# The opening of a two-block network on one core: first two products in a written order

## The chip, the core and the metric

The kernel runs on one core of a Trainium2 chip. A core has five engines with a queue each: TensorE (PE in the profile; its weight loads are PEld), VectorE (DVE), ScalarE (ACT), GpSimd (POOL) and SyncE (SP), which here only issues DMA transfers. An engine works off its queue in order; engines wait for each other through semaphores. The metric is device time in microseconds (us); times before are the median of three runs.

## The reference

The reference is a network of two blocks on 256 tokens of 1024 features, in float32, with its parameters as inputs. What matters here is its very first step, a norm and one wide product:

```python
def rmsnorm(x, g):
    xf = x.astype(jnp.float32)
    y = xf * lax.rsqrt(jnp.mean(xf * xf, axis=-1, keepdims=True) + RMS_EPS)
    return (y * g.astype(jnp.float32)).astype(x.dtype)
...
        h = rmsnorm(x, norm_mix_g[l])
        p = h @ w_in[l]
```

The columns of `p` go to a sliding-window attention, to a chunkwise mLSTM and to its gates; `w_out`, a cross attention with a second input `mem`, a gated feed-forward net, a second block (conformer convolution, sparse attention, two more feed-forward nets) and norms between them follow. All of that is unchanged.

## The kernel before

x lies transposed in SBUF, eight tiles of 128 features by 256 tokens (`self.x`, profile name `xres`). Weights come in chunks of 256 columns (`w_in` chunk 0, 1, 2, ...), each as two transfers of 512 KB into one of four raw buffers (`wraw`). To keep float32 accuracy at a faster matmul rate, every operand is split into a high part (a cast by ACT, L243 for weights and L325 for x) and a low part (the rest, by DVE, L246 and L326). A product is three matmuls: high by high, high by low, low by high (`mm3`, L263 to L265). One chunk is 8 tiles by 2 column halves by 3, that is 48 matmuls.

The norm's inverse root isn't applied to x. Products run on x times gain, and the root of the mean square, one number for each token, is multiplied in when a product leaves PSUM. It is made thus: the squares are summed over features, PE sums them over partitions (`zb`), DVE forms the mean (`rv`, L368), POOL takes the inverse root by 13 small instructions (`rsqrt`, `rs_n` and `rt_n`), PE spreads it over partitions (`bcb`, L375) and ACT copies that to SBUF (`bc_x`). DVE needs `bc_x` to evacuate the first products.

In the opening, `openB` and `norm` go through the eight tiles: split a tile, square it (ACT, or POOL for tiles 1, 3 and 5), let POOL add the squares up (`sqa`), and multiply the tile's rows of chunk 0. All transfers are issued by SP: the first gain columns of `par`, then weights and x in turn. The first mixer's steps (`MIX_AT`: chunks, gates, attention heads) are written in the order of a table of times. That is the order of the program; a scheduler may still move instructions of each engine's queue against it, outside of stretches marked `manual_schedule`, where the engines named keep the written order.

`w_in` chunk 2 holds the keys and values of the attention: DVE takes them out as `akT` and `avT`, and PE transposes `avT` (`bt`, L560). The gates' small product (`wgp`, from the transfer `gw`), the first attention scores (`bs`) and chunk 9 follow on PE.

Of the kernel before, what the change touches and what calls it, by code (L numbers as in the profile page):

```python
# [17 lines left out]
P = 128  # L18
# [113 lines left out]
class Net:  # L132
    def __init__(self, ctx, tc, T, dbg=None):
# [11 lines left out]

        nc.sync.dma_start(self.par[:, 0:KT], T["par"][:, 0:KT])
        self.early = [(self.x[:, m : m + 2, :], T["x"][:, m : m + 2, :]) for m in range(0, KT, 2)]
        self.early += [None, None, (self.ident, T["ident"]), (self.par[:, KT:], T["par"][:, KT:])]
# [18 lines left out]
    def plan(self, items):  # L167
        self.items = items
        self.stream = [(i, j) for i, item in enumerate(items) for j in range(len(self.sizes(item[0])))]
        self.data = [([], []) for _ in items]  # L170
        self.loaded = self.ready = self.used = 0
        self.run_ahead()
# [46 lines left out]
    def load(self, i, j):  # L219
        name, idx, _ = self.items[i]  # L220
        n = self.sizes(name)[j]
        raw = self.wp.tile([P, 1024], F32, name="wraw", tag="wraw", bufs=NRAW)[:, 0:n]
        self.nc.sync.dma_start(raw, self.T[name][idx][:, j * 1024 : j * 1024 + n])
        self.data[i][0].append(raw)
        for e in self.early[0:2]:
            if e:
                self.nc.sync.dma_start(*e)
        self.early = self.early[2:]
# [4 lines left out]
    def high(self, i, j):  # L233
        name, idx, k = self.items[i]
# [7 lines left out]
        hi, lo = both[:, 0, :], both[:, 1, :]  # L242
        self.nc.scalar.copy(hi, raws[j])  # L243

        def low():
            self.nc.vector.tensor_tensor(lo, raws[j], hi.bitcast(F32), op=ALU.subtract)  # L246
            pv = both.rearrange("p i (k c) -> p i k c", k=kh)
            prs.extend(pv[:, :, c, :] for c in range(kh))

        return low  # L250
# [23 lines left out]
    def linB(self, out, w, c0, c1, xx, nk=KT):  # L274
        for k in range(nk):
            self.mm3(out, w[k][:, :, c0:c1], xx[:, k], k == 0, k == nk - 1)

# [215 lines left out]
    def mixer(self, pool, mem):  # L493
# [29 lines left out]
        have, accs = set(), []  # L523
# [8 lines left out]
        def inp(c):  # L532
            nonlocal rb, rc
            if c == 0:
                b, step = self.openB(lambda: self.chunk("w_in", 0, room=0), xx)
                rc, _ = self.norm(lambda m: self.x[:, m, :], "g_mix", xx, step, (1, 3, 5))
                have.add("rc")
            elif c in (7, 8):
# [1214 lines left out]
```

## Time and profile before

| what | us |
|---|---|
| median of three runs (lowest, highest) | 1106.34 (1105.1, 1106.71) |
| the profiled execution | 1106.33 |
| its span, first to last instruction | 1104.5 |
| PE busy | 1063.6 (96%) |
| DVE busy | 803.6 (73%) |
| ACT busy | 598.2 (54%) |
| POOL busy | 138.9 (13%) |

The span is what the profile covers; the time of a run is a little longer. Busy is the time in which an engine had an instruction under way. PE's share leaves 40.9 us in which it stood. The profile's rows give start and duration, the engine, the line of the kernel, output and inputs by tile names, and, in brackets, how long the engine had been idle and what ended that.

### The profile page before, as it was taken

Reading aid. Unit: us, or ns where it says so; the run is one execution under the profiler, and the core shown is the slowest. Engines: PE = TensorE matmul, PEld = TensorE weight load, DVE = VectorE, ACT = ScalarE, POOL = GpSimd, SP = SyncE. Lnnn points to the kernel's source line nnn. Section 1 sums busy time; section 2 is a strip of 40 time slices with the busy share of each in tenths; the row PEclk is TensorE's granted clock in tenths of the full one; section 3 lists DMA queues with packets and bytes.
Section 4 is the critical chain, followed back from the end, with each engine's and each line's share of the span. In section 5 each row is a group of like instructions: output and inputs, shape, how many; then the busy total and the mean of one; then the engine's idle time right before and its main releaser. Section 6 shows DMA issues by size and latency. Waiting matters only on the chain.

```text
span 1104.5 us, 19673 instructions
## 1 busy us (share of the span) xinstructions
PE 1063.6 (96%) x7448; PEld 972.9 (88%) x7448; DVE 803.6 (73%) x1647; ACT 598.2 (54%) x1119; POOL 138.9 (13%) x343
## 2 busy tenths in 40 slices
PE   6899999999999999997789999999999999999998
PEld 6899999999999988885788888889999898888887
DVE  5886667768888865787877777765668748777763
ACT  5774556566666643311556666544365846666530
POOL 5120003012000000314030000012333103000000
PEclk9999999999999999998699999999999999999999
DMA  7744444435555654646165555755254034656670
GB/s 237 226 153 154 135 134 155 150 115 187 190 189 181 211 174 149 195 125 185 61 206 198 189 191 180 222 180 163 77 179 147 2 103 162 191 189 189 179 208 21
DMA packets 55414, 178.98 MB, mean 162 GB/s; under 512 B 9112, under 2 KB 11032, under 8 KB 55320
## 3 DMA queue, kind: packets, MB, share of 16 engines
q1 hardware_dynamic: 53400, 172.23, 49.3%
q0 software_dynamic: 1920, 5.50, 2.0%
q8 instruction: 58, 0.95, 0.3%
q14 instruction: 36, 0.29, 0.1%
HBM read 175.55 MB, written 2.16 MB: 161 GB/s over the span
## 4 chain that ended last, share of the span: by engine, by line
PE 84%; DVE 6%; DMA 3%; ACT 3%; POOL 2%; issue 2%; SPq 0%; ACTq 0%; DVEq 0%; POOLq 0%
PE pb L271 28%; PE pb L272 14%; PE pb L263 9%; PE pb L264 9%; PE pb L265 9%; PE pb L1034 3%; DVE cy L1096 2%; DMA wraw<-in_w_in_dram 1%; ACT wpr L243 1%; DVE wpr L246 1%; PE bt L1079 1%; PE bh L1357 1%; DVE xx L326 1%; DVE xres L443 1%; PE zb L1133 1%
## 5 line engine op out<-in xcount | busy, mean ns | idle before, releaser
L246 DVE TENSOR_TENSOR wpr<-wraw,wpr 128x1024 fp32r<-128x1024 f32 (+1 forms) x304 | 367.4, 1212 | 173.6 <-ACT wpr L243 171.0
L243 ACT CAST wpr<-wraw 128x1024 fp32r<-128x1024 f32 (+1 forms) x304 | 313.4, 1033 | 202.7 <-PE pb L272 95.1
L271 PE MATMUL pb<-xx,wpr 128*128 128x512 f32 x840 | 292.9, 392 | 0.0
L272 PE MATMUL pb<-xx,wpr 128*128 128x256 f32 x840 | 234.8, 280 | 0.0
L271 PEld LDWEIGHTS pb<-xx,wpr 128*128 128x128 f32 x840 | 157.7, 188 | 33.8
L271 PE MATMUL pb<-fhs,wpr 128*128 128x512 f32 x528 | 186.0, 394 | 0.0
L272 PEld LDWEIGHTS pb<-xx,wpr 128*128 128x128 f32 x840 | 157.8, 188 | 0.0
L272 PE MATMUL pb<-fhs,wpr 128*128 128x256 f32 x528 | 147.3, 279 | 0.0
L263 PE MATMUL pb<-xx,wpr 128*128 128x256 f32 x456 | 130.6, 290 | 8.7 <-ACT xx L325 8.6
L264 PE MATMUL pb<-xx,wpr 128*128 128x256 f32 x456 | 131.2, 288 | 2.5 <-DVE xx L326 2.4
L265 PE MATMUL pb<-xx,wpr 128*128 128x256 f32 x456 | 129.8, 285 | 0.0
L271 PEld LDWEIGHTS pb<-fhs,wpr 128*128 128x128 f32 x528 | 99.0, 187 | 23.2
L272 PEld LDWEIGHTS pb<-fhs,wpr 128*128 128x128 f32 x528 | 99.0, 188 | 0.0
L263 PEld LDWEIGHTS pb<-xx,wpr 128*128 128x128 f32 x456 | 87.5, 194 | 10.5 <-ACT xx L325 9.2
L264 PEld LDWEIGHTS pb<-xx,wpr 128*128 128x128 f32 x456 | 88.6, 194 | 4.0 <-DVE xx L326 3.3
L265 PEld LDWEIGHTS pb<-xx,wpr 128*128 128x128 f32 x456 | 88.5, 194 | 0.0
L263 PE MATMUL pb<-yy,wpr 128*128 128x256 f32 x256 | 74.0, 289 | 2.0 <-ACT yy L1175 2.0
L264 PE MATMUL pb<-yy,wpr 128*128 128x256 f32 x256 | 73.0, 285 | 0.0
L265 PE MATMUL pb<-yy,wpr 128*128 128x256 f32 x256 | 72.8, 285 | 0.0
L917 ACT COPY ft<-pb 128x256 f32<-128x256 f32 x105 | 38.7, 370 | 53.3 <-PE pb L272 53.3
L1096 DVE SCALAR_TENSOR_TENSOR cy<-cuz,par,cy 128x240 f32<-128x240 f32 (+14 forms) x120 | 55.2, 461 | 3.8
L263 PEld LDWEIGHTS pb<-yy,wpr 128*128 128x128 f32 x256 | 49.4, 193 | 2.4 <-ACT yy L1175 2.3
(422 smaller groups left out, 1952.4 us busy)
## 6 DMA issues: line engine op xcount, KB each, us to landing
wraw<-in_up_dram SPq DMA_DIRECT2D x44, 512.0 KB, 4.0
wraw<-in_up2a_dram SPq DMA_DIRECT2D x44, 512.0 KB, 4.4
wraw<-in_up2b_dram SPq DMA_DIRECT2D x44, 512.0 KB, 3.8
wraw<-in_w_in_dram SPq DMA_DIRECT2D x22, 512.0 KB, 4.5
wraw<-in_n_in_dram SPq DMA_DIRECT2D x20, 512.0 KB, 4.1
wraw<-in_wkv_dram SPq DMA_DIRECT2D x16, 512.0 KB, 4.2
wraw<-in_dn_dram SPq DMA_DIRECT2D x16, 512.0 KB, 3.7
wraw<-in_c_in_dram SPq DMA_DIRECT2D x16, 512.0 KB, 4.0
```

The source lines that it names most:

```text
L243: self.nc.scalar.copy(hi, raws[j])
L246: self.nc.vector.tensor_tensor(lo, raws[j], hi.bitcast(F32), op=ALU.subtract)
L263: mm(out, left[:, 0], right[:, 0], start=start, stop=False, skip_group_check=True)
L264: mm(out, left[:, 0], right[:, 1], start=False, stop=False, skip_group_check=True)
L265: mm(out, left[:, 1], right[:, 0], start=False, stop=stop, skip_group_check=True)
L271: mm(out, left[:, 0], right, start=start, stop=False, skip_group_check=True)
L272: mm(out[:, 0], left[:, 1], right[:, 0], start=False, stop=stop, skip_group_check=True)
L326: nc.vector.scalar_tensor_tensor(lo, src, g, hi.bitcast(F32), op0=ALU.mult, op1=ALU.subtract)
L443: self.nc.vector.tensor_tensor(self.x[:, m, :], acc[m // 2][:, (m % 2) * S : (m % 2) * S + S], self.x[:, m, :], op=ALU.add)
L917: nc.scalar.copy(t, b[:, 1])
L1034: nc.tensor.matmul(b, raw[k // 4][:, k % 4, c], xg[:, k, :], start=(k == 0), stop=(k == KT - 1))
L1096: nc.vector.scalar_tensor_tensor(y, us[m][:, 0 : S - t], tap(m, t), y, op0=ALU.mult, op1=ALU.add)
```

## The change

The first two products get a function of their own, `opening`, under `manual_schedule` for PE, DVE and ACT. x and the first columns of `par` are issued by ACT. PE multiplies 18 times a cleared tile. The first weight is split in halves, and within chunk 0 all high-by-high matmuls of four tiles come first, then high by low, then low by high. Chunk 1 follows, then the squares: all by ACT, each summed by PE at once (16 matmuls in place of 4), and the root is asked for behind that. The preloading of weights no longer begins in `plan`.

```diff
@@ -142,10 +142,6 @@
         self.x = self.cp.tile([P, KT, S], F32, name="xres")
         self.par = self.cp.tile([P, NPAR], F32, name="par")
         self.ident = self.cp.tile([P, P], F32, name="ident")
-        nc.sync.dma_start(self.par[:, 0:KT], T["par"][:, 0:KT])
-        self.early = [(self.x[:, m : m + 2, :], T["x"][:, m : m + 2, :]) for m in range(0, KT, 2)]
-        self.early += [None, None, (self.ident, T["ident"]), (self.par[:, KT:], T["par"][:, KT:])]
         self.ones = self.cp.tile([P, 1], F32, name="ones")
         nc.vector.memset(self.ones, 1.0)
         self.zero = self.cp.tile([P, 1], F32, name="zero")
@@ -169,7 +165,6 @@
         self.stream = [(i, j) for i, item in enumerate(items) for j in range(len(self.sizes(item[0])))]
         self.data = [([], []) for _ in items]
         self.loaded = self.ready = self.used = 0
-        self.run_ahead()
 
     @staticmethod
     def sizes(name):
@@ -222,15 +217,17 @@
         raw = self.wp.tile([P, 1024], F32, name="wraw", tag="wraw", bufs=NRAW)[:, 0:n]
         self.nc.sync.dma_start(raw, self.T[name][idx][:, j * 1024 : j * 1024 + n])
         self.data[i][0].append(raw)
-        for e in self.early[0:2]:
-            if e:
-                self.nc.sync.dma_start(*e)
-        self.early = self.early[2:]
 
     def convert(self, i, j):
         self.high(i, j)()
 
     def high(self, i, j):
+        both, raw = self.pair(i, j)
+        self.nc.scalar.copy(both[:, 0, :], raw)
+        return lambda: self.nc.vector.tensor_tensor(both[:, 1, :], raw, both[:, 0, :].bitcast(F32), op=ALU.subtract)
+    def pair(self, i, j):
         name, idx, k = self.items[i]
         n = self.sizes(name)[j]
         kh = n // P if name[:2] == "dn" else k // 2
@@ -239,15 +236,9 @@
             both = self.fp.tile([P, 2, 1024], F32R, name="wfi", tag="wfi", bufs=2)
         else:
             both = self.wp.tile([P, 2, 1024], F32R, name="wpr", tag="wpr", bufs=NHI)[:, :, 0:n]
-        hi, lo = both[:, 0, :], both[:, 1, :]
-        self.nc.scalar.copy(hi, raws[j])
-        def low():
-            self.nc.vector.tensor_tensor(lo, raws[j], hi.bitcast(F32), op=ALU.subtract)
-            pv = both.rearrange("p i (k c) -> p i k c", k=kh)
-            prs.extend(pv[:, :, c, :] for c in range(kh))
-        return low
+        pv = both.rearrange("p i (k c) -> p i k c", k=kh)
+        prs.extend(pv[:, :, c, :] for c in range(kh))
+        return both, raws[j]
 
     def chunk(self, name, idx, **ahead):
         assert self.items[self.used][:2] == (name, idx), (self.items[self.used], name, idx)
@@ -274,6 +265,76 @@
     def linB(self, out, w, c0, c1, xx, nk=KT):
         for k in range(nk):
             self.mm3(out, w[k][:, :, c0:c1], xx[:, k], k == 0, k == nk - 1)
+    def opening(self, gname):
+        nc, T = self.nc, self.T
+        mm = nc.tensor.matmul
+        nc.gpsimd.memset(self.yy[:, 0, 0].bitcast(F32), 0.0)
+        b, cold = [self.bank(), self.bank()], self.bank()
+        zb = self.zbank()
+        engines = {mybir.EngineType.PE, mybir.EngineType.DVE, mybir.EngineType.Activation}
+        with self.tc.manual_schedule(engines=engines):
+            nc.scalar.dma_start(self.par[:, 0:KT], T["par"][:, 0:KT])
+            for m in range(0, KT, 2):
+                nc.scalar.dma_start(self.x[:, m : m + 2, :], T["x"][:, m : m + 2, :])
+            while self.loaded < NRAW:
+                self.load(*self.stream[self.loaded])
+                self.loaded += 1
+            nc.sync.dma_start(self.ident, T["ident"])
+            nc.sync.dma_start(self.par[:, KT:], T["par"][:, KT:])
+            for _ in range(18):
+                mm(cold[:, 0:S], self.yy[:, 0, 0, 0:P], self.yy[:, 0, 0], start=True, stop=True)
+            w = self.data[0][1]
+            def weights(p, halves):
+                both, raw = self.pair(*self.stream[p])
+                n = raw.shape[1] // halves
+                cs = [slice(i * n, i * n + n) for i in range(halves)]
+                for c in cs:
+                    nc.scalar.copy(both[:, 0, c], raw[:, c])
+                    yield
+                for c in cs:
+                    nc.vector.tensor_tensor(both[:, 1, c], raw[:, c], both[:, 0, c].bitcast(F32), op=ALU.subtract)
+                    yield
+                self.ready += 1
+            def rows(m):
+                self.split_g(self.x[:, m, :], self.col(gname, m), self.xx[:, m])
+            def products(ks):
+                for lo, ro in ((0, 0), (0, 1), (1, 0)):
+                    for k in ks:
+                        for i in range(2):
+                            mm(b[i][:, 0:S], w[k][:, lo, i * P : i * P + P], self.xx[:, k, ro],
+                               start=(k == 0 and lo + ro == 0), stop=(k == KT - 1 and lo == 1), skip_group_check=True)
+            first = weights(0, 2)
+            next(first)
+            rows(0)
+            rows(1)
+            next(first)
+            rows(2)
+            rows(3)
+            for _ in first:
+                pass
+            for _ in weights(1, 1):
+                pass
+            products(range(4))
+            for m in range(4, KT):
+                rows(m)
+            products(range(4, KT))
+            for p in (2, 3):
+                for _ in weights(p, 1):
+                    pass
+            self.data[0], self.used = None, 1
+            second = self.linB1(self.chunk("w_in", 1, room=0), self.xx)
+            for m in range(KT):
+                self.colsum(zb, self.square(self.x[:, m, :]), m)
+        v = self.meansq(zb[:, 0:NT])
+        return [b[0][:, 0:S], b[1][:, 0:S]], second, self.rsqrt(v, NT, "n")
 
 
 
@@ -520,7 +581,7 @@
         mo = pool.tile([P, 4, S], F32, name="mo")
         to = [None] * 4
         rb = rc = None
-        have, accs = set(), []
+        have, accs, ahead = set(), [], {}
 
         def need(*keys):
             while not have.issuperset(keys):
@@ -532,9 +593,10 @@
         def inp(c):
             nonlocal rb, rc
             if c == 0:
-                b, step = self.openB(lambda: self.chunk("w_in", 0, room=0), xx)
-                rc, _ = self.norm(lambda m: self.x[:, m, :], "g_mix", xx, step, (1, 3, 5))
+                b, ahead[1], rc = self.opening("g_mix")
                 have.add("rc")
+            elif c in ahead:
+                b = ahead[c]
             elif c in (7, 8):
                 b = self.lin2A(self.chunk("w_in", c), xx)
             else:
```

What the change moves in the queues is seen at two places. The first is the head of SP's queue, the transfers in the order in which they are issued; before:

```order
L146 DMA par<-in_par_dram 128x8
L223 DMA wraw<-in_w_in_dram 128x1024
L227 DMA xres<-in_x_dram 128x512 x2
L223 DMA wraw<-in_w_in_dram 128x1024
L227 DMA xres<-in_x_dram 128x512 x2
L223 DMA wraw<-in_w_in_dram 128x1024 x2
L227 DMA ident<-in_ident_dram 128x128
L227 DMA par<-in_par_dram 128x493
```

and now:

```order
L565 DMA gb<-in_gate_b_dram 4x2
L563 DMA gw<-in_gate_w_dram 128x8x4 x2
L567 DMA abias<-in_abias_dram 128x384
L569 DMA tri<-in_tri_st_dram 128x256
L218 DMA wraw<-in_w_in_dram 128x1024 x4
L286 DMA ident<-in_ident_dram 128x128
L287 DMA par<-in_par_dram 128x493
L1277 DMA pos<-in_positions_dram 128x2
```

x (`xres`) and the first piece of `par` are gone to ACT; the mixer's constants (`gb`, `gw` twice, `abias`, `tri`), which stood behind these rows and more weights, now stand ahead of the first weight.

The second is PE's queue between the product of `w_in` chunk 1 and that of chunk 2 (both show as `pb<-xx,wpr`), with the spread of the root, `bcb`, between them; before:

```order
L264 MATMUL pb<-xx,wpr 128x256
L265 MATMUL pb<-xx,wpr 128x256
L263 MATMUL pb<-xx,wpr 128x256
L264 MATMUL pb<-xx,wpr 128x256
L265 MATMUL pb<-xx,wpr 128x256
L375 MATMUL bcb<-ident,rs_n 128x128 x2
L263 MATMUL pb<-xx,wpr 128x256
L264 MATMUL pb<-xx,wpr 128x256
L265 MATMUL pb<-xx,wpr 128x256
```

and now, where the last row of chunk 1 stands ahead of the sums:

```order
L254 MATMUL pb<-xx,wpr 128x256
L255 MATMUL pb<-xx,wpr 128x256
L256 MATMUL pb<-xx,wpr 128x256
L401 MATMUL zb<-ones,sq 128x1 x16
L436 MATMUL bcb<-ident,rs_n 128x128 x2
L254 MATMUL pb<-xx,wpr 128x256
L255 MATMUL pb<-xx,wpr 128x256
L256 MATMUL pb<-xx,wpr 128x256
```

The sums of squares (`zb`) stood among the matmuls of chunks 0 and 1, with the rest of chunk 1 between them and `bcb`; now all 16 stand behind chunk 1, with nothing between them and `bcb`.

## Rows read from the trace of the kernel before

**Rows 1.** Stages of the opening: busy time by engine, granted clock, DMA share and rate.

```profile
core 0: us, PE busy (x) PEld busy (x) DVE busy (x) ACT busy (x) POOL busy (x), PEclk, DMA share, GB/s
...
6.82:13.18 6.36, 3.88 (x14) 3.00 (x14) 4.88 (x6) 3.88 (x10) 3.25 (x5) 1.00 1.02 376
13.18:18.89 5.71, 5.71 (x26) 5.71 (x27) 5.71 (x6) 5.23 (x9) 4.56 (x5) 1.00 0.47 177
18.89:26.71 7.82, 7.82 (x66) 7.61 (x65) 4.99 (x11) 2.63 (x7) 4.82 (x13) 1.00 0.68 215
...
33.27:36.14 2.87, 0.00 (x1) 0.01 (x1) 2.87 (x7) 1.96 (x5) 0.98 (x2) 0.99 0.71 226
36.14:39.56 3.42, 3.42 (x16) 2.93 (x17) 3.10 (x6) 2.14 (x3) 0.00 (x0) 0.51 0.71 244
...
41.68:100.00 58.32, 58.32 (x479) 57.16 (x479) 44.55 (x121) 37.67 (x71) 6.55 (x18) 1.00 0.55 173
```

**Rows 2.** SP's queue in order of time: start, duration, transfers issued.

```profile
1.19 0.42 SPq L223 DMA_DIRECT2D wraw<-in_w_in_dram  x1
...
23.68 0.65 SPq L502 DMA_DIRECT2D gw<-in_gate_w_dram  x1
...
28.34 0.55 SPq L502 DMA_DIRECT2D gw<-in_gate_w_dram  x1
28.94 0.60 SPq L504 DMA_DIRECT2D gb<-in_gate_b_dram  x1
29.58 0.47 SPq L506 DMA_DIRECT2D abias<-in_abias_dram  x1
30.10 0.42 SPq L508 DMA_DIRECT2D tri<-in_tri_st_dram  x1
```

**Rows 3.** ACT in order of time, first 21 us.

```profile
0.74 1.28 ACT L243 ACT_TABLE_LOAD   x1 [0.74 <-PEq L1742]
5.21 1.04 ACT L243 CAST wpr<-wraw 128x1024 fp32r<-128x1024 f32 x1 [3.18 <-DMA wraw<-in_w_in_dram]
...
12.72 0.50 ACT L325 ACTIVATE xx<-xres,par 128x256 fp32r<-128x256 f32 x1
13.12 1.03 ACT L243 CAST wpr<-wraw 128x1024 fp32r<-128x1024 f32 x1
```

**Rows 4.** DVE in order of time, first 21 us.

```profile
12.17 3.46 DVE L326 SCALAR_TENSOR_TENSOR xx<-xres,par,xx 128x256 fp32r<-128x256 f32 x4
...
18.10 1.21 DVE L246 TENSOR_TENSOR wpr<-wraw,wpr 128x1024 fp32r<-128x1024 f32 x1
19.23 0.47 DVE L326 SCALAR_TENSOR_TENSOR xx<-xres,par,xx 128x256 fp32r<-128x256 f32 x1
```

**Rows 5.** POOL in order of time, first 27 us: the chain of 13 instructions.

```profile
1.06 0.17 POOL L568 MEMSET mu<- 128x3 f32 x3
...
20.90 1.25 POOL L351 TENSOR_SCALAR rs_n<-rv 128x2 int32<-128x2 int32 x1 [3.00 <-DVE rv L368]
...
26.61 0.20 POOL L360 TENSOR_TENSOR rs_n<-rs_n,rt_n 128x2 f32<-128x2 f32 x1
```

**Rows 6.** The same chain in the last norm.

```profile
921.04 1.11 POOL L351 TENSOR_SCALAR rs_n<-rv 128x2 int32<-128x2 int32 x1 [2.22 <-DVE rv L368]
...
926.25 0.20 POOL L360 TENSOR_TENSOR rs_n<-rs_n,rt_n 128x2 f32<-128x2 f32 x1
```

**Rows 7.** PE in order of time, first 28 us.

```profile
20.25 0.36 PE L424 MATMUL zb<-ones,sq 128*128 128x1 f32 x2
...
26.86 0.71 PE L375 MATMUL bcb<-ident,rs_n 128*128 128x128 f32 x4 [0.15 <-POOL rs_n L360]
```

**Rows 8.** PE in order of time, 32.9 to 42 us.

```profile
36.14 0.69 PE L560 MATMUL bt<-ident,avT 128*128 128x128 f32 x2 [2.87 <-DVE avT L530]
...
41.68 0.38 PE L263 MATMUL pb<-xx,wpr 128*128 128x256 f32 x1
```

**Rows 9.** PE in order of time, squares summed in an earlier norm.

```profile
386.74 0.50 PE L463 MATMUL zb<-g,sq 128*128 128x2 f32 x4
387.11 0.48 PE L271 MATMUL pb<-fhs,wpr 128*128 128x512 f32 x1
```

## The prediction

> **What bounds the kernel now.** I read the table of stages first, then the chain of waits, then the engines in order of time over the first 42 us. Over the whole span TensorE (PE) is busy for 96%, so an edit pays only where PE stands or runs slowly. The table of stages [rows 1] shows where that is in the opening. Until 6.82 us PE does nothing. From 6.82 to 13.18 it works 3.88 of 6.36 us, while the DMA engines are full (share 1.02, 376 GB/s). From 13.18 to 18.89 it works without a gap, but 26 records take 5.71 us; from 18.89 on 66 take 7.82 us. That is 0.22 and 0.118 us for a product of 256 columns, which fit TensorE's 1.2 and 2.4 GHz. The clock column says 1.00 in both, so here the pace tells more than the column. At 33.27 PE stands 2.87 us for the transposes of v, and after it 16 records take 3.42 us (0.214 each, granted clock 0.51). From 41.68 to 100 it works 58.32 of 58.32 us. So the place to reckon to is 41.68, the first matmul of `w_in` chunk 9 [rows 8]: what PE is late or early there it still is at 100.
>
> One thing costs nothing today and decides the forecast: the inverse root of the norm, 13 POOL instructions from 20.90 to 26.81 [rows 5]. PE's last sum of squares ends at 20.61, the broadcast `bcb` that needs the root starts at 26.86 [rows 7]. In those 6.25 us PE multiplies chunk 1; it stands for the root only 0.15 us.
>
> **The change part by part.**
>
> *SP's queue.* x (4 issues) and the first 4 KB of `par` leave it. But SP isn't among the engines held in the written order, and five constants of the mixer now stand ahead of the first weight. By their rows these issues take 0.60 + 0.65 + 0.55 + 0.47 + 0.42 = 2.69 us [rows 2]. Starting with the program at 0.74, as ACT does [rows 3], the first weight is issued at 3.43 instead of 1.19, 2.24 us later. Before, it was cast at 5.21; moved by 2.24 that is 7.45, the early bound. `abias` and `tri` (320 KB) lie ahead of it on SP's queue; at 376 GB/s they take 0.87 us, which makes 8.3. If all of x (1 MB, 2.8 us at that rate) went ahead as well, 11.1 would be the late bound; x has been running since about 1.2, so most of it is past. I take 8.2.
>
> *x on ACT's queue.* No row shows a DMA issued by ACT; by SP's rows an issue takes 0.42 to 0.65 us of the issuing engine. ACT has nothing else to do then, so I cost it at nothing; without that cover it would be five issues, about 2 us. The engines are full from 6.82 [rows 1], so a second queue can't add bandwidth there. The Trainium skill, "DMA: Bandwidth & Descriptors", section "Issuing engines are not separate DMA queues", says the same against this edit: DMAs from several engines run on the same 16 engines and interleave, and a second queue saves only issue time. By that rule the sum stays as it is; the trace before has one issuing queue only and can't show it.
>
> *ACT's front.* The cast of the gate weights (`wgp`) now stands ahead of all weight casts, waits for both `gw` transfers, and takes the table load along: 1.28 us [rows 3], and a cast of 288 columns that I put below half of the 1.04 us for 1024. `gw` is issued by 2.6, so this is done near 7.5 and hidden behind the first weight; if `gw` lands late, each us past 6.5 is a us lost.
>
> *Zeros.* 18 products of zeros start when POOL has cleared `yy`, about 1.4 us (its last small memset started at 1.06 [rows 5]), and at 0.214 us end near 5.3. PE then stands until about 9.2. In the rows a stand of 2.87 us was followed by the low pace [rows 1], so I give the zeros no gain. The Trainium skill, "TensorE: Matmul & The Clock Gate", section "What's actually happening", says that throttled is the default state and activity releases it; by that alone the zeros would lift the clock for the first product. That result is a rival below.
>
> *High parts first, squares off POOL and late.* From 8.2 ACT casts half a weight (0.5), splits x rows at a pitch of 0.40 (12.72 to 13.12 [rows 3]), and the first product can start at 9.25. DVE's low parts are later than ACT's high parts. With POOL idle I take the undisturbed 0.47 for a low split, 0.40 apart when they follow each other as ACT's do, against 3.46/4 = 0.87 beside POOL's squares, and 1.21 for a weight [rows 4]. Two rows of x to 10.05; the next two wait for ACT and end at 11.4; weight 0 to 12.6, weight 1 to 13.8, four rows to 15.4, weights 2 and 3 to 17.8. PE's 48 products of chunk 0 start at 9.25; all at 0.214 they would end at 19.5. In the rows the faster pace came 3.4 to 5.7 us into a stretch without gaps, so I let it come at 15: they end at 17.7. Chunk 1 is 48 x 0.118 = 5.7 us, to 23.4 (22.0 if only weight 3's low part at 17.8 and the 36 products behind it count; 24.9 at the late bound of the clock and half a us of DMA). Before, chunk 1 ended at 26.6, so up to here 3.2 us are gained.
>
> *Sums of squares on PE.* 16 small matmuls behind chunk 1 instead of 4. Two of that kind took 387.11 - 386.74 = 0.37 us [rows 9], so 8 x 0.37 = 3.0, to 26.4. POOL's additions go, which were off PE's path.
>
> *The root.* This is the step that costs. In PE's new order `bcb` stands right behind the sums, and all of chunk 2 behind `bcb`. Nothing covers POOL's 13 instructions any more. From the last sum to `bcb` I take 6.2 us: 6.25 in this norm [rows 7]; 5.41 instead of 5.91 us of chain in the last one [rows 6] would make it 5.75. `bcb` starts at 32.6, against 26.86: 5.7 us late.
>
> *Behind it.* `bcb` takes 0.46 us, chunk 2 takes 48 x 0.118 = 5.66 plus 16 x (0.214 - 0.118) = 1.54 for the clock lost in 6 us of standing (before, PE ran through here): it ends at 40.2. Then the transposes of v wait on DVE for `akT`, the low part of a weight that now stands between (1.21), and `avT`: about 2.0 us, to 42.2; before they began at 36.14. From there to chunk 9 it was 5.54 us [rows 8], 1.54 of it clock; I take 5.0. Chunk 9 starts at 47.2 instead of 41.68: **5.5 us later**. The weights of chunk 9 are cast by then, so nothing new waits.
>
> The profiled execution took 1106.33 us (span 1104.5), like the median of the runs, 1106.34. The sum is 1106.33 + 5.5 = **1111.8 us**.
>
> **The rivals.**
> - *Zeros keep the clock.* For it: PE is busy for 3.9 us just before. Against it: the row after 2.87 us of standing. Chunk 1 would end at DVE's bound, 22.0 instead of 23.4: 1110.4.
> - *Weights later still.* x and the weights share the engines, and the second to fourth weight wait for `gw` and x in SP's queue. For it: DMA share 1.02 in the opening. Against it: x is asked for first. With the first weight at 9.9, 1.7 us more: 1113.5.
> - *Early data (not slower).* One mechanism: the constants pass in less time than their rows say, the first weight is there at 5.2 as before, and the zeros run straight into the products. Then DVE ends weight 3 at 14.8 and chunk 1 at 19.0 instead of 23.4, 4.4 us less: 1107.4, no change. It decides if the first cast starts before 5.7. Against it: five issues ahead, each with a row.
> - *A shift is swallowed later.* PE stands 40.9 us in all (1104.5 - 1063.6), 28 of them after 42 us. Where a transfer and not PE's own chain sets such a stand, lateness costs nothing there: up to 3 us back, 1108.8. Against it: 58 us without a gap come first.
> - *The change doesn't do what it says.* If the order as built were of no effect on PE's wait, `bcb` would start at once after the sums; no row gives such a root under 5.4 us.
>
> **How the numbers follow.** The forecast 0.56, weights later 0.17, the clock kept 0.12, swallowed 0.08, early data 0.07. 0.2% is 2.2 us, about what a measurement of this kernel tells from no change. Slower by more: all but early data and a part of swallowed, 0.90. Within it 0.07. Faster 0.03: early data and a swallowed shift together. The range: below, the early end of the opening (-1.4), of the root (-0.5) and of the clock behind it (-1.0) make 1108.9; above, weights 1.7 later and the clock low for longer in chunk 2 (+1.1) and in the gates (+0.5) make 1115.1. I take 1108.8 to 1115.2.
>
> **What the new profile would show.** Zeros from 1.4 to 5.3; the first weight cast near 8.2; chunk 1 done near 23.4, earlier than 26.6; then a stand of PE of about 6 us before `bcb`, released by POOL's root; after it a stretch at a granted clock near 0.5; the transposes of v near 42; chunk 9 near 47. The forecast is wrong if `bcb` starts before 29, or if the 5.5 us at chunk 9 are no longer there at the end.

## The result and the profile after

The changed kernel took 1116.71 us (median of 4 runs, 1116.36 to 1117.91) against 1105.72 us before (4 runs beside them): ratio 1.0101, 95% interval 1.0084 to 1.0119. It is slower, as forecast, but by 11 us where 5.5 were forecast, and outside the range. The profiled execution has a span of 1114.6 us, against 1104.5.

The difference is there when the opening ends. TensorE (PE) in order of time, changed kernel (start, duration, what, in brackets the standing before and what ended it):

```profile
1.42 3.64 PE L289 MATMUL pb<-yy 128*128 128x256 f32 x18 [1.42 <-POOL mu L630]
12.43 8.61 PE L311 MATMUL pb<-xx,wpr 128*128 128x256 f32 x48 [7.37 <-ACT xx L386]
...
26.51 3.63 PE L401 MATMUL zb<-ones,sq 128*128 128x1 f32 x32
35.84 1.22 PE L436 MATMUL bcb<-ident,rs_n 128*128 128x128 f32 x4 [5.70 <-POOL rs_n L421]
...
46.87 0.44 PE L622 MATMUL bt<-ident,avT 128*128 128x128 f32 x2 [1.98 <-DVE avT L591]
...
50.90 0.39 PE L254 MATMUL pb<-xx,wpr 128*128 128x256 f32 x1
```

Before, `bcb` started at 26.86 [rows 7], the transposes at 36.14 and chunk 9 at 41.68 [rows 8]. Chunk 9 is 9.2 us late. Behind it the shift stays: the root of the next norm starts at 194.14 us, against 184.96 before, 9.2 us later. The remaining 1 to 2 us of the 11 arise further on; where is open.

Stages of the changed kernel (busy time by engine, granted clock, DMA share, GB/s), to be laid beside [rows 1]:

```profile
core 0: us, PE busy (x) PEld busy (x) DVE busy (x) ACT busy (x) POOL busy (x), PEclk, DMA share, GB/s
...
5.06:12.43 7.37, 0.01 (x1) 0.00 (x0) 0.47 (x2) 2.79 (x5) 0.00 (x0) 0.68 1.05 289
12.43:18.00 5.57, 5.47 (x24) 5.18 (x25) 5.14 (x10) 5.57 (x11) 0.00 (x0) 0.51 0.72 243
...
30.14:35.84 5.70, 0.00 (x0) 0.00 (x0) 2.51 (x4) 1.68 (x4) 4.43 (x14) 0.62 0.48 156
35.84:41.91 6.07, 6.07 (x28) 6.07 (x29) 3.56 (x6) 4.49 (x10) 4.29 (x6) 0.51 0.33 115
...
44.89:46.87 1.98, 0.00 (x0) 0.00 (x0) 1.94 (x4) 1.28 (x2) 0.00 (x0) 1.00 0.58 157
46.87:50.90 4.03, 4.03 (x31) 3.51 (x31) 3.44 (x3) 2.71 (x3) 0.00 (x0) 1.00 0.71 209
...
50.90:109.22 58.32, 58.32 (x479) 57.16 (x479) 41.22 (x103) 33.78 (x67) 7.89 (x18) 1.00 0.50 164
```

Two stands are seen: 7.37 us for the first data, with the DMA engines full (1.05) at only 289 GB/s, and 5.70 us for the root. After each, a stretch at half clock follows (0.51). From chunk 9 on PE works 58.32 of 58.32 us, exactly as before.

The head of the two DMA queues, SP's first and then ACT's, answers to [rows 2]; the third part, ACT's first work, to [rows 3]:

```profile
1.19 1.34 SPq L563 DMA_DIRECT2D gw<-in_gate_w_dram  x2
2.58 2.13 SPq L567 DMA_DIRECT2D abias<-in_abias_dram  x1
4.75 0.43 SPq L569 DMA_DIRECT2D tri<-in_tri_st_dram  x1
5.23 3.23 SPq L218 DMA_DIRECT2D wraw<-in_w_in_dram  x4
```

```profile
0.74 0.39 ACTq L280 DMA_DIRECT2D par<-in_par_dram  x1
1.16 4.12 ACTq L282 DMA_DIRECT2D xres<-in_x_dram  x4
7.43 1.28 ACT L391 ACT_TABLE_LOAD   x1 [7.43 <-DMA gw<-in_gate_w_dram]
8.72 0.43 ACT L391 CAST wgp<-gw 128x288 fp32r<-128x288 f32 x1
11.35 0.62 ACT L297 CAST wpr<-wraw 128x512 fp32r<-128x512 f32 x1 [2.20 <-DMA wraw<-in_w_in_dram]
```

`abias` alone took 2.13 us to issue, against 0.47 [rows 2]. (ACT's group of four holds a gap: three pieces of x are issued by 2.6, the fourth at 4.95.) The first weight was issued at 5.23 and cast at 11.35; the forecast had 3.43 and 8.2.

### The profile page after: what moved, and what is told of

The parts are those of the page before. It is cut to its first block, busy times and chain, and to the rows that moved or that the text cites. A ratio compares the mean times of both kernels' runs of the same rounds, so it can differ in the third digit from the quotient of the medians.

```text
span 1114.6 us, 19745 instructions
## 1 busy us (share of the span) xinstructions
PE 1069.8 (96%) x7490; PEld 980.1 (88%) x7490; DVE 801.9 (72%) x1649; ACT 600.3 (54%) x1123; POOL 131.2 (12%) x335
## 3 DMA queue, kind: packets, MB, share of 16 engines
q10 hardware_dynamic: 720, 1.05, 0.3%
## 4 chain that ended last, share of the span: by engine, by line
PE 85%; DVE 6%; ACT 3%; DMA 2%; POOL 2%; issue 1%; SPq 0%; ACTq 0%; POOLq 0%; DVEq 0%
PE pb L262 28%; PE pb L263 14%; PE pb L254 10%; PE pb L255 10%; PE pb L256 10%; PE pb L1096 3%; DVE cy L1158 2%; DVE wpr L227 1%; PE bt L1141 1%; ACT wpr L226 1%; PE bh L1419 1%; DVE xx L387 1%; PE pb L311 1%; PE zb L1195 1%; DVE xres L504 1%
## 5 line engine op out<-in xcount | busy, mean ns | idle before, releaser
L227 DVE TENSOR_TENSOR wpr<-wraw,wpr 128x1024 fp32r<-128x1024 f32 (+1 forms) x300 | 361.3, 1207 | 167.7 <-ACT wpr L226 164.8
L226 ACT CAST wpr<-wraw 128x1024 fp32r<-128x1024 f32 (+1 forms) x300 | 309.2, 1034 | 199.6 <-PE pb L263 97.2
L263 PE MATMUL pb<-xx,wpr 128*128 128x256 f32 x840 | 234.8, 280 | 0.0
L262 PEld LDWEIGHTS pb<-xx,wpr 128*128 128x128 f32 x840 | 157.7, 188 | 33.7
L263 PEld LDWEIGHTS pb<-xx,wpr 128*128 128x128 f32 x840 | 157.8, 188 | 0.0
L254 PE MATMUL pb<-xx,wpr 128*128 128x256 f32 x440 | 125.7, 288 | 1.3 <-ACT xx L386 1.3
L255 PE MATMUL pb<-xx,wpr 128*128 128x256 f32 x440 | 125.5, 286 | 0.1
L256 PE MATMUL pb<-xx,wpr 128*128 128x256 f32 x440 | 124.7, 284 | 0.0
L254 PEld LDWEIGHTS pb<-xx,wpr 128*128 128x128 f32 x440 | 84.3, 193 | 2.8 <-ACT xx L386 1.5
L255 PEld LDWEIGHTS pb<-xx,wpr 128*128 128x128 f32 x440 | 84.8, 193 | 1.1 <-DVE xx L387 0.3
L256 PEld LDWEIGHTS pb<-xx,wpr 128*128 128x128 f32 x440 | 84.7, 192 | 0.0
```

What stands on the lines that cost most here:

```text
L226: self.nc.scalar.copy(both[:, 0, :], raw)
L227: return lambda: self.nc.vector.tensor_tensor(both[:, 1, :], raw, both[:, 0, :].bitcast(F32), op=ALU.subtract)
L254: mm(out, left[:, 0], right[:, 0], start=start, stop=False, skip_group_check=True)
L255: mm(out, left[:, 0], right[:, 1], start=False, stop=False, skip_group_check=True)
L256: mm(out, left[:, 1], right[:, 0], start=False, stop=stop, skip_group_check=True)
L262: mm(out, left[:, 0], right, start=start, stop=False, skip_group_check=True)
```

## The experiments

All are compared with the kernel before, run beside them on the same chip (its medians there 1104.8 to 1106.1). What the runs are read by is the start of chunk 9, since single runs scatter by 2 us and more. Each start is read from one profiled execution, the times are medians. What lies behind chunk 9 took 1060.8 to 1065.0 us in the executions of this table, so a shift at chunk 9 is found in the time only to within some 2 us.

| kernel | first product | `bcb` | transposes | chunk 9 | us | ratio to before, 95% |
|---|---|---|---|---|---|---|
| before | 6.82 | 26.86 | 36.14 | 41.68 | 1105.7 | 1 |
| changed | 12.43 | 35.84 | 46.87 | 50.90 | 1116.7 | 1.0084 to 1.0119 |
| e1 constants behind the weights | 8.17 | 33.69 | 44.36 | 49.93 | 1115.8 | 1.0063 to 1.0120 |
| e10c x on SP | 9.94 | 32.79 | 42.72 | 46.72 | 1112.7 | 1.0043 to 1.0094 |
| e10 both | 6.38 | 33.16 | 43.08 | 48.64 | 1113.8 | 1.0062 to 1.0096 |
| e2 sums and root ahead of chunk 1 | 12.66 | 31.67 | 43.16 | 49.54 | 1115.3 | 1.0059 to 1.0115 |
| e12 = e1 and e2 | 8.14 | 28.36 | 39.55 | 45.89 | 1111.2 | 1.0031 to 1.0068 |
| e5 = e10 and e2 | 6.78 | 27.59 | 36.86 | 42.41 | 1106.5 | 1.0001 to 1.0029 |
| e8 = e5, root on DVE | 6.46 | 26.25 | 34.94 | 40.49 | 1105.5 | 0.9995 to 1.0028 |
| e11 = e8, 24 zeros | 6.75 | 27.73 | 36.31 | 40.33 | 1104.8 | 0.9982 to 1.0005 |

### Where the late start comes from: x's queue and the constants

e10c: x back on SP's queue, nothing else.

```diff
-            nc.scalar.dma_start(self.par[:, 0:KT], T["par"][:, 0:KT])
-            for m in range(0, KT, 2):
-                nc.scalar.dma_start(self.x[:, m : m + 2, :], T["x"][:, m : m + 2, :])
+            nc.sync.dma_start(self.par[:, 0:KT], T["par"][:, 0:KT])
             while self.loaded < NRAW:
                 self.load(*self.stream[self.loaded])
                 self.loaded += 1
+                if self.loaded < 3:
+                    for m in (4 * self.loaded - 4, 4 * self.loaded - 2):
+                        nc.sync.dma_start(self.x[:, m : m + 2, :], T["x"][:, m : m + 2, :])
```

> The changed kernel with x back on SP's queue between the weights, but the mixer's constants still ahead of all of it. Theory (two queues that issue at once make each issue and each landing slower, so the constants alone cost little more than their issues): the constants' issues take 0.4 to 0.65 us each as in the kernel before, first weight issued near 4.0, cast near 8.0, first product near 9.6; chunk 9 about 3 us later than in e10, about 1112.5 us. Rival (the constants' transfers themselves are slow, with one queue too): abias is issued for 2 us and more again, first product near 12, about 1116 us.

SP's queue in e10c, then ACT's first work and PE:

```profile
1.19 1.36 SPq L564 DMA_DIRECT2D gw<-in_gate_w_dram  x2
2.59 0.66 SPq L568 DMA_DIRECT2D abias<-in_abias_dram  x1
3.29 0.43 SPq L570 DMA_DIRECT2D tri<-in_tri_st_dram  x1
3.76 0.43 SPq L280 DMA_DIRECT2D par<-in_par_dram  x1
4.24 0.43 SPq L218 DMA_DIRECT2D wraw<-in_w_in_dram  x1
4.71 0.91 SPq L286 DMA_DIRECT2D xres<-in_x_dram  x2
```

```profile
4.91 1.28 ACT L392 ACT_TABLE_LOAD   x1 [4.91 <-DMA gw<-in_gate_w_dram]
...
8.51 0.62 ACT L298 CAST wpr<-wraw 128x512 fp32r<-128x512 f32 x1 [1.88 <-DMA wraw<-in_w_in_dram]
9.38 0.91 ACT L387 ACTIVATE xx<-xres,par 128x256 fp32r<-128x256 f32 x2 [0.25 <-DMA xres<-in_x_dram]
```

```profile
9.94 8.09 PE L312 MATMUL pb<-xx,wpr 128*128 128x256 f32 x48 [4.31 <-ACT xx L387]
...
32.79 1.23 PE L437 MATMUL bcb<-ident,rs_n 128*128 128x128 f32 x4 [5.67 <-POOL rs_n L422]
...
46.72 0.38 PE L254 MATMUL pb<-xx,wpr 128*128 128x256 f32 x1
```

The theory's first half came out: with one queue `abias` is issued in 0.66 us, `gw` is there at 4.91 instead of 7.43, the first weight is cast at 8.51 instead of 11.35, though SP now has x to issue too. Moving x to a second queue costs 2.5 us at the first product and 4.2 at chunk 9. The median, 1112.7, is the expected one; that chunk 9 would be 3 us later than in e10 was wrong (it is 1.9 us earlier, see e10).

The traces also show what passed on the two queues. When the first weight was issued in the changed kernel, at 5.23, 0.61 of x's 1.05 MB had moved on ACT's queue, and on SP's queue only 0.02 MB: `gw` consists of 2,048 packets of 16 bytes, and x's packets went between them. From issue to landing `gw` took 5.4 us, `abias` 5.2 and `tri` 3.3, against 2.7, 2.7 and 2.3 in e10c. So the last constant ahead of the weight was in near 8.1 us instead of 5.6: that is 2.5 of the 2.84 us by which the first cast is later.

e1: x stays on ACT's queue, and the mixer's four constants (`gw` in two pieces) are issued behind the weights; the same five lines go from where they stood.

```diff
                 b, ahead[1], rc = self.opening("g_mix")
+                for i in range(2):
+                    nc.sync.dma_start(gw[:, :, 32 * i : 32 * i + 4], T["gate_w"][:, :, 4 * i : 4 * i + 4])
+                nc.sync.dma_start(gb, T["gate_b"])
+                nc.sync.dma_start(bias, T["abias"])
+                nc.sync.dma_start(tri, T["tri_st"])
```

> The changed kernel (1116.7 us), but the mixer's constants (gw, gb, abias, tri) are issued behind the weights, and so the cast of the gate weights leaves the front of ACT. Theory (the constants on SP's queue made the first weight late, the root's wait is a separate term): the first weight is issued near 1.2 us instead of 5.23 and cast near 6.3 instead of 11.35; all of the opening moves up by 5 us; the wait of TensorE before bcb stays at 5.7 us; about 1111.7 us. Rival (the weight was late because the DMA engines carried 1 MB of x beside it, from a second queue): it lands only when x has passed, near 8.5, 2.9 us earlier: about 1113.8 us.

ACT's first work in e1:

```profile
1.18 2.49 ACTq L282 DMA_DIRECT2D xres<-in_x_dram  x4
3.70 1.28 ACT L297 ACT_TABLE_LOAD   x1 [3.70 <-issue]
4.99 0.62 ACT L297 CAST wpr<-wraw 128x512 fp32r<-128x512 f32 x1
7.61 0.91 ACT L386 ACTIVATE xx<-xres,par 128x256 fp32r<-128x256 f32 x2 [2.00 <-DMA xres<-in_x_dram]
...
10.37 0.91 ACT L386 ACTIVATE xx<-xres,par 128x256 fp32r<-128x256 f32 x2 [1.35 <-DMA xres<-in_x_dram]
```

Neither side was right as put. The weight is there by 4.99, but now x is late: its pairs are split at 7.61 and 10.37, against 5.82 and 8.52 in e10, where they stand in SP's queue. x is issued sooner on its own queue (the first piece at 1.18, in e10 at 1.66) and lands later: all four weights, of which three aren't needed yet, run beside it. On one queue the order w, x, x, w, x, x, w, w is the order of need; two queues give that up. The first product came 4.3 us earlier, chunk 9 only 1.0. The rest went on the way: waits in chunk 0 (1.54 us for x) and in the sums leave 2.2 us at `bcb` and 2.5 at the transposes, and the stretch from there to chunk 9 took 5.57 us at a mean clock of 0.69, against 4.03 at 1.00.

e10: both edits.

> The changed kernel with x back on SP's queue between the weights and the constants behind them; squares, sums and the uncovered root stay as changed. With the changed kernel, e1_weights_first and the next run this makes a square of two edits. Theory (the late data cost some 6 us at the first product, and the uncovered root the rest): first product near 6.8 us as before, chunk 1 done near 21, bcb near 30, TensorE still stands 5.7 us for the root; chunk 9 near 45 instead of 50.9, about 1110 us, as in the forecast of an uncovered root alone. Rival (the root's wait is swallowed where TensorE waits for avT): chunk 9 near 42.4, as in e5_x_on_sync, about 1106.5 us.

The first product starts at 6.38, earlier than in any other run, and chunk 1 is done at 21.7, 4.8 us before the changed kernel. `bcb` is only 2.7 us earlier, at 33.16, where I had expected 30, and the time 1113.8 us instead of 1110. Two waits took the gain, ACT's first:

```profile
20.92 1.71 ACT L387 ACTIVATE mm<-wraw,par 128x256 fp32r<-128x256 f32 x4 [2.14 <-DMA wraw<-in_mem_dram]
23.25 0.51 ACT L387 ACTIVATE mm<-wraw,par 128x256 fp32r<-128x256 f32 x1 [0.62 <-DMA wraw<-in_mem_dram]
23.67 2.02 ACT L448 ACTIVATE sq<-xres 128x256 f32<-128x256 f32 x5
```

Five squares of x stand in ACT's queue behind the splits of the second input `mem`, whose transfer lands at 20.9. And on POOL additions of squares of `mem` got in between the root's instructions: PE stood 6.65 us for it. The rival, chunk 9 near 42.4, was further off still. From the transposes to chunk 9 it took 5.56 us at a mean clock of 0.69, against 4.00 at 1.00 in e10c.

### What the root costs

e2: squares, sums and root ahead of chunk 1, so that chunk 1 covers the root.

```diff
             self.data[0], self.used = None, 1
-            second = self.linB1(self.chunk("w_in", 1, room=0), self.xx)
             for m in range(KT):
                 self.colsum(zb, self.square(self.x[:, m, :]), m)
-        v = self.meansq(zb[:, 0:NT])
-        return [b[0][:, 0:S], b[1][:, 0:S]], second, self.rsqrt(v, NT, "n")
+            v = self.meansq(zb[:, 0:NT])
+            root = self.rsqrt(v, NT, "n")
+            second = self.linB1(self.chunk("w_in", 1, room=0), self.xx)
+        return [b[0][:, 0:S], b[1][:, 0:S]], second, root
```

> The changed kernel, but the squares, their sums and the root stand ahead of w_in chunk 1, so that chunk 1 covers the 13 POOL instructions of the root. Theory (the uncovered root costs its whole length, and the clock behind it): bcb near 30.3 us instead of 35.84, and chunk 2 at 0.118 us for each matmul, 24 of which took 0.21 (2.3 us): 8 us less, about 1108.7 us. Rival 1 (the low clock in chunk 2 has another cause): only the 5.5 us, about 1111.2 us. Rival 2 (ACT squares too slowly, TensorE now waits for the squares instead): 3 us less, about 1113.7 us.

PE in e2, and the stretch behind the sums by stages:

```profile
20.92 3.63 PE L402 MATMUL zb<-ones,sq 128*128 128x1 f32 x32
...
31.67 0.60 PE L437 MATMUL bcb<-ident,rs_n 128*128 128x128 f32 x4
...
43.16 0.69 PE L623 MATMUL bt<-ident,avT 128*128 128x128 f32 x2 [5.18 <-DVE avT L592]
```

```profile
20.92:24.41 3.49, 3.49 (x34) 3.49 (x33) 1.85 (x7) 2.89 (x7) 0.00 (x0) 1.00 0.80 270
24.41:27.71 3.30, 3.30 (x18) 3.30 (x18) 3.09 (x13) 2.78 (x8) 2.38 (x7) 0.51 0.63 195
27.71:31.67 3.96, 3.96 (x34) 3.96 (x34) 1.44 (x7) 1.02 (x3) 3.31 (x10) 0.98 0.39 138
```

The stand before `bcb` is gone, and `bcb` is 4.2 us earlier, not 5.5: behind the 16 sums PE has a low clock for 3.3 us (0.51), though it never stood. At the transposes PE then stands 5.18 us for `avT`. None of the three cases put a stand there: PE is through chunk 2 earlier, but from `bcb` to the transposes it takes 11.5 us, as in the changed kernel (11.0), so these are still 3.7 us earlier (43.16 for 46.87). What shrinks the gain is the clock behind the new stand: from the transposes to chunk 9 it took 6.38 us at a mean of 0.59, against 4.03 at 1.00, and chunk 9 is only 1.4 us earlier. In the chain behind it ACT stood 3.46 us for POOL, which did the root while the additions for `mem` waited; the next weights then came late (two of ACT's casts waited for their transfers, 0.98 and 1.24 us), and `avT` on DVE stands behind those weights' low parts. That POOL is what made them late is tested by e8.

e12: e1 and e2 together.

> Weights first on SP's queue, and sums and root ahead of chunk 1. Theory (the two terms add up): 5 us and 8 us less than the changed kernel, about 1103.7 us, some 2 us under the kernel before. Rival (with data earlier, DVE's low parts of the weights set the pace of chunk 0 and swallow part of it): about 1106 us, no change against the kernel before.

45.89 at chunk 9: 5.0 us earlier than the changed kernel, where the single edits gave 1.0 and 1.4. Each alone is mostly swallowed, at different places (e1 in chunk 0 and the clock behind the transposes, e2 in that clock). Together `bcb` and the transposes came 7.5 and 7.3 us earlier, where the single edits add up to 6.3 and 6.2; PE again stood for `avT` (4.88 us), and the clock behind that stand (0.59) took 2.3 us back. The expected 1103.7 was missed by 7.5 us.

e5: e12 with x back on SP, the diff of e10c.

> The kernel with weights first and sums first (1111.2 us), and x back on SP's queue between the weights, as in the kernel before. Theory (two queues share the same engines, so the four weights and x arrive together and late: there the first weight was cast at 5.16 us, but the first product waited for x to 8.14): first product near 7 us, second pair of x without the 1.2 us wait of ACT, chunk 9 of w_in 1 to 2 us earlier, about 1109.5 us. Rival (the second queue does bring x and weights sooner together, since SP alone issues them one by one): chunk 9 not earlier, 1111.2 us or more.

First product at 6.78, chunk 9 at 42.41: 3.5 us earlier than e12 and more than expected, 1106.5 us. With that the loss against the kernel before is all but gone.

e7 and e8: the root on DVE (`self.rsqrt(v, NT, "n", nc.vector)`), once alone in the changed kernel, once in e5.

> The changed kernel with only the root of the first norm on VectorE instead of GpSimd, still uncovered behind the sums. Theory (TensorE's 5.7 us of standing are the length of the 13 GpSimd instructions): with 11 VectorE instructions of 0.1 to 0.2 us bcb starts some 3.5 us earlier, near 32.3 us, about 1113 us. Rival (VectorE's low parts of weights, 1.2 us each, get in between, or the shift is lost at the transposes of v): chunk 9 less than 1.5 us earlier, 1115.5 us or more.

The rival was right: `bcb` came at 37.05, 1.2 us later, and PE stood 6.52 us; chunk 9 at 51.40, 1116.2 us (1.0076 to 1.0137). DVE in e7:

```profile
30.77 0.17 DVE L412 TENSOR_SCALAR rs_n<-rv 128x2 int32<-128x2 int32 x1
...
31.45 1.23 DVE L227 TENSOR_TENSOR wpr<-wraw,wpr 128x1024 fp32r<-128x1024 f32 x1
32.59 0.68 DVE L417 TENSOR_TENSOR rt_n<-rs_n 128x2 f32<-128x2 f32 x1
...
36.84 0.16 DVE L424 SCALAR_TENSOR_TENSOR rs_n<-rt_n,rs_n 128x2 f32<-128x2 f32 x1
```

Instructions of 0.16 us, with other work put between them: 6.2 us in all.

> As e5_x_on_sync, with the root of this first norm on VectorE instead of GpSimd. Theory (POOL's root holds up POOL's sums of the second input's squares, ACT stood 3.3 us for those, the raw buffers of weights came free late, and TensorE stood 4.9 us for avT behind them): ACT's wait goes, TensorE's wait for avT falls to about 2 us, chunk 9 some 3 to 4 us earlier than in e5, about 1106 us. Rival (the weights are late for want of DMA rate, not of buffers): no change against e5.

ACT's wait fell from 3.2 to 0.4 us, PE's wait for `avT` from 3.03 to 2.35, chunk 9 from 42.41 to 40.49. The direction is as expected, the gain at chunk 9 about half of it; the times (1105.5 and 1106.5 us, whose intervals overlap) don't tell the two apart.

e14, e13, e15, e16: is it the place of `bcb` in PE's queue? One row of the table of times puts chunk 2 ahead of `bcb` and the gates ahead of the transposes (e14 in the changed kernel, e13 in e11, e15 in e11 with the squares added and the root taken by POOL again and four sums behind chunk 1, e16 in the kernel before).

```diff
-    (-1.679, 2.88, "in", 0), (0.028, 1.05, "in", 1), (1.229, 0.42, "in", 2), (3.379, 0.5, "mem"),
+    (-1.679, 2.88, "in", 0), (0.028, 1.05, "in", 1), (1.19, 1.3, "in", 2), (3.379, 0.5, "mem"),
```

> The changed kernel with one row of the table of times altered: chunk 2 of w_in now stands ahead of bcb in TensorE's queue, and the gates' product ahead of the transposes of v. Theory (the root costs its 5.7 us only because chunk 2 waits behind it): TensorE's stand before bcb is gone or under 1 us, the high clock holds, and chunk 9 starts near 43 instead of 50.9, about 1109 us. Rival (VectorE and ScalarE are then the last: they need bc_x for six products, and the low parts of weights lie between): TensorE stands 3 us or more elsewhere before chunk 9, which starts at 47 or later, 1113 us or more.

> As e11_zeros_24 (1104.8 us), with the same row of the table altered. Theory: the gates' product (3.2 us) covers the wait for avT (2.3 us), and chunk 9 starts near 38 instead of 40.3, about 1102.5 us. Rival (the next weights are not cast by then): no change.

> As e13, but the squares are added by GpSimd again, summed by 4 small matmuls of TensorE behind chunk 1 instead of 16 ahead of it, and the root is on GpSimd again, covered by chunk 2. Theory (the 16 small matmuls cost TensorE 4 us and the clock of the product behind them, 2.7 us more): chunk 0, 1 and 2 run through to about 28 us, chunk 9 starts near 33 to 35, about 1099 us. Rival (the weights of chunk 2 and 9 come no sooner, since casts and low parts set the pace): TensorE waits for weights inside chunk 2 or 9, chunk 9 at 38 or later, 1102.5 us or more.

> The kernel before with only the same row of the table altered. Theory (there TensorE stood 2.87 us for the transposes and had the low clock in the gates, 1.5 us): the gates' product covers the stand, chunk 9 starts near 38 instead of 41.68, about 1102 us. Rival (the root was covered there already, and VectorE is late in any order): chunk 9 as before, 1105.7 us.

PE in e14:

```profile
38.61 0.71 PE L436 MATMUL bcb<-ident,rs_n 128*128 128x128 f32 x4 [1.72 <-POOL rs_n L421]
39.08 0.36 PE L254 MATMUL pb<-xx,wgp 128*36 128x256 f32 x1
49.49 0.66 PE L622 MATMUL bt<-ident,avT 128*128 128x128 f32 x2 [7.40 <-DVE avT L591]
```

The theory fell, the rival came true. With `bcb` out of chunk 2's way PE stood 7.40 us for `avT` instead; chunk 9 at 51.65, 1121.1 us (1.0119 to 1.0162). e13 and e15 became slower than e11 too, 1111.1 and 1112.7 us, which neither side had forecast (1102.5 and 1099): PE stood 5.22 and 6.30 us for `avT`. In e15 PE had ended chunk 2 at 27.93, 5.5 us ahead of e13, and chunk 9 was no earlier for it (43.82 and 44.09). e16 didn't change (1104.7, 0.9995 to 1.0021). From the start of `bcb` to the transposes it takes 10.9 us in e14, 11.0 in the changed kernel, 11.5 in e2, 9.9 in e10c, 9.3 before, 8.7 in e8, and 8.6 in e11 and e13, which differ in that row of the table alone: the path behind the root goes through ACT's copy of it and six products on DVE between low parts of weights, and the changed order hardly alters it. So what counts is when the root is there, and what DVE has in between.

### What the zeros do

e3: the changed kernel without zeros. e4: with 68. e8n and e11: e8 without, and with 24 (there the first product starts at 6.5 to 6.9).

> The changed kernel without the 18 products of zeros. Theory (the zeros are over 7 us before the data and do nothing): 1116.7 us, the first product at the same time and at the low clock, granted clock near 0.5 from it to about 17.8 us, as with the zeros. Rival (the zeros shorten the low stretch of chunk 0): chunk 0 ends 1 to 2 us later, about 1118 us.

> The changed kernel with 68 products of zeros instead of 18, which reach almost to the data (18 of them end at 5.06 us, the first product starts at 12.43). Theory (18 zeros end too early, the clock is low again by the first product): with 68 the first product finds the high clock, chunk 0 takes 6.5 to 7 us instead of 8.45 and chunk 1 ends 1.5 us earlier, about 1115 us. Rival (zeros don't raise the clock, or the low parts by DVE set the pace of chunk 0): no change, 1116.7 us.

> As e8_root_on_vector (1105.5 us), without zeros. Theory (18 zeros, then 1.2 us of standing, then the products: they do help here): the high clock comes later in chunk 0, chunk 9 some 1 to 2 us later, about 1107 us. Rival (zeros never matter): no change, 1105.5 us.

> As e8_root_on_vector (1105.5 us), with 24 zeros instead of 18, which end just when the first product can start (18 ended at 5.29, the first product started at 6.46). Theory (zeros count only where they reach to the data): the high clock comes some 2 us earlier in chunk 0, chunk 9 up to 1.5 us earlier, about 1104.5 us. Rival (ACT and DVE set the pace of chunk 0 once data are there): no change.

In the changed kernel 18 zeros end at 5.06, 7.4 us too early: without them chunk 0 took 8.80 us instead of 8.61. (e3's median, 1120.6 us, ratio 1.0084 to 1.0174, stands on four runs from 1114.3 to 1123.0; the profiled one, at 1114.3, shows no reason for the others. Its interval overlaps the changed kernel's, so the zeros' worth there isn't settled by time.) With 68 that reach to the data, chunk 1 ended at 25.6 instead of 26.5, 0.9 of the expected 1.5; but PE then waited 2.93 us for ACT's squares, `bcb` came at 39.68, and the time is the same (1116.1). In e8 the 44 products took 7.99 us without zeros, 6.86 with 18, 6.53 with 24, and chunk 9 started at 40.47, 40.49 and 40.33. The granted clock over them was 0.77 with 18 zeros and 1.00 with 24; without zeros the first 26 took 5.70 us, 0.22 each, the pace of the lower level. So zeros that ended 1.2 and 0.7 us ahead of the first product made the rest of chunk 0 faster, those that ended 7.4 us ahead hardly; and the gain was swallowed up to chunk 9 again. The 1 to 1.5 us that e8n and e11 should have differed by in time aren't there (1105.8, 1105.5, 1104.8 us).

No version is clearly faster than the kernel before. e11 is 12 us faster than the changed kernel; against the kernel before it is 0.9993, an interval that holds 1.

## Why the prediction was wrong

The forecast's own steps, beside the changed kernel and e10c, which differs from it in the queue of x and of `par`'s first piece alone:

| step | forecast | changed | e10c |
|---|---|---|---|
| first weight cast | 8.2 | 11.35 | 8.51 |
| first product | 9.25 | 12.43 | 9.94 |
| chunk 0 ends | 17.7 | 20.88 | 18.03 |
| chunk 1 ends | 23.4 | 26.51 | 23.49 |
| sums end | 26.4 | 30.14 | 27.12 |
| `bcb` | 32.6 | 35.84 | 32.79 |
| chunk 2 ends | 40.2 | 44.89 | 41.6 |
| transposes | 42.2 | 46.87 | 42.72 |
| chunk 9 | 47.2 | 50.90 | 46.72 |
| time | 1111.8 | 1116.7 | 1112.7 |

**The step that failed** is "x on ACT's queue ... I cost it at nothing", with its sentence in the step before, "x has been running since about 1.2, so most of it is past". The first cast came 3.15 us late (11.35 for 8.2), and 2.84 of them are gone in e10c. I priced ACT's time for five issues and the rate of full engines, but not that x on a second queue delays what lies in the first. Nor was most of x past: at 3.43, where I put the first weight's issue, 0.20 of its 1.05 MB had moved. Against e10c `abias` took 1.5 us longer to issue, `gw` was 2.5 us later (7.43, 4.91), and the first weight was cast 6.1 us after its issue instead of 4.3. Of the 2.84 us between the casts (11.35 and 8.51), 1.0 is issue and 1.8 landing. With one queue my terms hold to within 0.7 us down to `bcb`, and the sum to 0.9 us. Behind `bcb` that agreement is partly luck: chunk 2 ended 1.4 us later than forecast, and the stand before the transposes and the gates gave 1.9 back.

The whole miss of 4.9 us adds up so: 3.2 at `bcb`, all of it there at the first product; 1.5 more in chunk 2; 1.0 less from the transposes to chunk 9; and 1.2 behind chunk 9, where I had put nothing.

The bounds were there: 7.45 and 11.1, and it came out at 11.35, just past the end at which all of x goes first. I took 8.2 near the early end and gave the rival "weights later still" only 1.7 us. A price between ends 3.6 us apart should have been carried into the range, which ended at 1115.2.

The Trainium skill, "DMA: Bandwidth & Descriptors", section "Issuing engines are not separate DMA queues", says that DMAs of several engines interleave on the same 16 engines and that a second queue saves issue time only. The runs agree on the interleaving, and show the other side: giving up the one queue's order cost 4.2 us at chunk 9 (e10c). Issue time wasn't saved at the first weight: it was issued at 5.23 with two queues and at 4.24 with one.

**Right**: the weights are late because the constants stand ahead of them (cast at 5.10 in e10, at 8.51 in e10c, which differ in that alone). Chunk 0 took 8.45 us as forecast, chunk 1 5.63 for 5.7. (By the paces that I named, chunk 0 would have ended at 17.5 and not at 17.7, 0.2 us that stayed in the sum; and 24.9, given as a late bound for chunk 1, follows from no row named, but isn't used further.) The uncovered root was right in place and size: 5.70 us for 6.2, released by POOL, and shown by e2, where it goes.

**Off in size**: the sums took 3.6 us for 3.0. I had taken the price from the sums of another norm; in this one a sum took 0.22 us already before, from 20.03 to 20.25 and from there to the next product at 20.48, and 16 of them make 3.5. ACT didn't set that pace: its squares waited for PE (0.28 us in the changed kernel). The low clock behind the root lasted 6.07 us with 28 records (35.84 to 41.91) where I had 16 products: `bcb` and chunk 2 took 9.05 us for 7.6. I put that clock down to the stand; in e2 it came behind the sums without any stand, so which of the two brought it here is open. The gates took 4.03 for 5.0, since a stand of 1.98 us didn't cost the clock this time (1.00).

**Rivals**: that the zeros keep the clock was wrong here, since 7.37 us of standing followed them (granted clock 0.51 from 12.43 to 18.00). "Weights later still" is what happened, with 3.15 us where I gave it 1.7. "Early data" would have needed one queue and the constants behind the weights: the first product was at 6.38 only with both (e10). A swallowed shift was wrong for what comes after 42 us, but within the opening swallowing is the rule (e1, e2, e10).

Open: what the slower landing of the constants would have been without `gw`'s small packets was not tried; nor what made the issue of `abias` long (2.08 to 2.33 us in all six kernels with x on ACT's queue and the constants first); nor what let the clock survive one 2 us stand and not another.

## What to carry to other kernels

A second DMA queue isn't free even where the issuing engine has nothing to do: ask what in the first queue it will run beside, and keep data that are needed in an order in one queue. When a chain hangs on a small serial computation, price the engines that consume its result, too: covering the root moved `bcb` by 4.2 us, the transposes by 3.7 and, with the clock that the new stand cost, chunk 9 by 1.4 (e2). Judge edits of an opening together: early data and a covered root moved chunk 9 by 2.3 and 1.4 us alone (e10, e2) and by 8.5 us together (e5).

## What the hardware showed beside that

16 sums with one column each kept PE busy for 3.6 us, and the products right behind ran at half clock for 3.3 us (0.51 in e2, no gap before them); the same is seen in all seven kernels with these sums ahead of chunk 1, while four such sums, in the kernel before and in e15, left no such stretch. The issue of one transfer, `abias`, lasted 0.66 us or over 2 us by what the other queue did.
